# Where the weight sums of the seven-product projections are made: in advance in DRAM, or on POOL as they are used

## The chip, the cores and the metric

The kernel runs on one core of one Trainium2 chip. The metric is the device time of one execution in microseconds (us), the median of three runs. PE is TensorE, DVE is VectorE, ACT is ScalarE, POOL is GpSimd, SP is SyncE, which issues the DMAs here.

## The reference

One inference step of a two-layer trunk, all in float32. The prompt is one sequence of 2048 tokens, the sample is 8 sequences of 8 tokens with stored states; the model width is 1024.

```python
# layer 0: gated DeltaNet (8 heads, 128 x 128 states), chunked
# layer 1: retention
p = rmsnorm(x) @ w_in                       # 1024 -> 1024 q, 1024 k, 2048 v, 2048 gate
q, k = rotary(q), rotary(k) * 256 ** -0.5   # 4 heads, dk 256, dv 512
# per head, chunkwise:  S_t = gamma_h S_{t-1} + k_t^T v_t ;  o_t = q_t S_t
o = rmsnorm(o) * silu(gate)
y = x + o @ w_out
# then a final rmsnorm; outputs: y, and the states of both layers
```

The change touches layer 1 alone, and in it the input projection of q, k, v and gate.

## The kernel before

Layer 0 comes first; it ends near 1500 us. Layer 1 then goes over four blocks of 512 prompt tokens (n = 0 to 3) and, in each, over four heads (h = 0 to 3). Block 0 carries the 64 sample columns as well (width 576). For each head the order of the main line is: gate projection, q, k, then v, then the output projection of the head before (outproj_B), while the retention of the head before (ret_prompt, four chunks of 128 tokens; in block 0 then ret_sample) is interleaved with the gate, q and k projections. The final norm of a block (final) is put after its head 3.

Float32 products are made on PE as three passes of a high and a low part (PASSES). A weight is therefore split before use: ACT copies it to the high part, DVE subtracts to get the low part (split, L209 to L211, or wload for 128x1024 tiles, L195 to L197). Split weights go into a ring of three `w` tiles (wtile), raw ones come through two `wraw` buffers.

Blocks below FIRST7 (0 and 1) project plainly (colproj, pv). From FIRST7 on the projection of two output halves from two input halves, a quad of weight quarters A11, A12, A21, A22, is made with seven products in place of eight. Their right sides are sums of the activations (build_halves: b11, t1, t2, b21, t3, b22, n4; the sums use tags "ta", "tb" and "tc"); their left sides are, in this order, x = 0 (A11), 4 (A21 + A22), 5 (that less A11), 1 (A12), 6 (A11 - A21), 7 (A12 less number 5) and 3 (A22). `seven` puts the products together: two ACT copies, five DVE adds that read PSUM, two POOL adds. A head has four quads of q, k and gate (t = 0 to 3; quad, 12 matmuls of 256 columns for a product) and two of v (t = 4, 5, interleaved; vquad).

The four sums of each quad are made in advance: prep(u), two tasks of low priority (u = 0, 1, half the columns each) that begin after the projections of head 0 in block 0, load each quad, make four sums on POOL, split them (ACT L1055, DVE L1056) and store them to wh_d in DRAM. Each has 24 pieces (4 heads x 6 quads), and before the first build_halves the main line waits for both tasks (pipe.wait(*ptask)). wstream then loads x >= 4 split from wh_d (512 KB each), and x = 0, 1, 3 raw, which it splits.

The order of work has two makers. _Pipe interleaves generator tasks with the main line as the program is written out, by an estimate of PE time and by priority. A planner then orders each engine's instructions by that order of priority and by its own costs, and gives tiles their buffers: tiles of one tag share its buffers, and a buffer passes on when all uses of the former tile are done, those written later included. On the chip each engine, and SP's queue, goes through its list in order.

Tags that matter: in block 0 the pool `pb` holds p0 and p1 (QRs, KRs of the sample), p2 (first vraw, the sample's values, L1548, read by eight small loads at L1257; then K3, written at L1275, read until the last Kts, L1321), raws (raw q and k of the sample). In later blocks p0 to p2 are the second half of the ring of residual tiles (xst, six buffers), taken after pipe.wait(lastret).

Of the kernel before, what the change touches and what calls it, by code (L numbers as in the profile page):

```python
# [10 lines left out]
F32 = mybir.dt.float32  # L11
F32R = mybir.dt.float32r
AF = mybir.ActivationFunctionType
ALU = mybir.AluOpType
# [5 lines left out]
BH = 4  # L20
# [61 lines left out]
class _Layer:  # L82
    pb = None
# [8 lines left out]
def tile_hybrid(ctx: ExitStack, tc: tile.TileContext, a: dict, S: int):  # L92
    nc = tc.nc
    V, ACT, PL = nc.vector, nc.scalar, nc.gpsimd
# [47 lines left out]
    x1_d = dr.tile([D, S + NS], F32, name="x1_d")  # L142
    x2_d = dr.tile([D, S + NS], F32, name="x2_d")
    sr_d = dr.tile([BH, 128, 1024], F32, name="sr_d")
    wh_d = [dr.tile([24, 128, 1024], F32, name=f"wh_d{h}") for h in range(BH)]

    def const(name, shape, src, pool=cst):
        t = pool.tile(list(shape), F32, name=name)
# [26 lines left out]

    def xst(name, wide=True):
        if not wide and xn_[1] == 6:
            k = xn_[2] % 6
            xn_[2] += 1
            if k >= 3:  # L180
                return B.pb.tile([128, TB], F32, tag=f"p{k - 3}", name=name)
        else:
            k = xn_[0] % min(xn_[1], 3 if B.pb else 4)
            xn_[0] += 1
        return (pa if k == 3 else sb).tile([128, XC], F32, tag=f"xst{k}", name=name)
# [829 lines left out]
    def quarters(src, vkind):  # L1015

        if vkind:
            q = [[v3(src[j], 512)[:, :, 256 * i : 256 * i + 256] for i in range(2)] for j in range(2)]
            return q[0][0], q[1][0], q[0][1], q[1][1]
        return [src[j][:, 512 * i : 512 * i + 512] for j in range(2) for i in range(2)]  # L1020
# [16 lines left out]
    def prep(u):  # L1037

        pb = B.pb
        tag = ("ta", "tb")[u]  # L1040
        for h, t in ((h, t) for h in range(BH) for t in range(6)):
            src, vkind = quads(h)[t]
            R = pb.tile([128, 4, 256], F32R, tag=tag, bufs=2, name="Rw")
            Sm = pb.tile([128, 4, 256], F32, tag=tag, bufs=2, name="Sm")
            A11, A12, A21, A22 = (R[:, i, :].bitcast(F32) for i in range(4))
            for x, y in zip((A11, A12, A21, A22), halves_of(src, vkind, u)):
                nc.sync.dma_start(x, y)
            yield 10.0
            PL.tensor_tensor(Sm[:, 0], A21, A22, op=ALU.add)
            PL.tensor_tensor(Sm[:, 1], Sm[:, 0], A11, op=ALU.subtract)  # L1050
            PL.tensor_tensor(Sm[:, 2], A11, A21, op=ALU.subtract)  # L1051
            PL.tensor_tensor(Sm[:, 3], A12, Sm[:, 1], op=ALU.subtract)
            yield 10.0
            with behind():
                ACT.copy(R, Sm)  # L1055
                V.tensor_tensor(Sm.bitcast(F32R), Sm, R.bitcast(F32), op=ALU.subtract)  # L1056
            yield 8.0
            out = wh_d[h][4 * t : 4 * t + 4].rearrange("x p (l v c) -> p x l v c", l=2, v=2)[:, :, :, u, :]
            nc.sync.dma_start(out[:, :, 0], R.bitcast(F32))
            nc.sync.dma_start(out[:, :, 1], Sm)  # L1060
            yield 8.0

    def wstream(h):

        q = quads(h)
        jobs = []
        for ts in ([0], [1], [2], [3], [4, 5]):
            for x in (0, 4, 5, 1, 6, 7, 3):
                jobs += [(t, x) for t in ts]
        for i in range(0, len(jobs), 2):  # L1070
            w, raw = wtile(), None
            for j, (t, x) in enumerate(jobs[i : i + 2]):
                o = w[:, j, :]
                src, vkind = q[t]
                if x < 4:
                    if raw is None:
                        raw = sb.tile([128, 1024], F32, tag="wraw", bufs=2, name="wraw")
                    d = raw[:, 512 * j : 512 * j + 512]
                    nc.sync.dma_start(v3(d, 256) if vkind else d, quarters(src, vkind)[x])
                    split(o[:, :512], o[:, 512:], d)  # L1080
                else:
                    nc.sync.dma_start(o.bitcast(F32), wh_d[h][4 * t + x - 4])
            for j in range(2):
                yield v3(w[:, j, :], 512)

# [97 lines left out]
    def ret_prompt(n, h, QR, KR, Vt, GT, OG, S_):  # L1183
        pb = B.pb
        gC = float(gam[h] ** 128)
        rmask = pb.tile([128, 128], F32, tag="rmk", bufs=2, name="rmk")
        nc.sync.dma_start(rmask, a["rmask"][:, h, :])
        for c in range(4):
            tk = slice(c * 128, (c + 1) * 128)
# [56 lines left out]
    def ret_sample(h, QRs, KRs, vraw, GTs, OG):  # L1246
# [52 lines left out]
        for half in range(2):  # L1299
            o = po("os")  # L1300
            mm(o, Ash[:, half * 128 : (half + 1) * 128], V3[:, half], start=True, stop=False)
            for k in range(2):
                yield LAT_ST
                i0 = 8 * half + 4 * k
                t = pipe.t

                def query(b4):
                    r = slice(32 * b4, 32 * b4 + 32)
                    return mm(o[r], QRs[:, k, half * 128 + 32 * b4 : half * 128 + 32 * b4 + 32], loads[i0 + b4],
                              start=False, stop=(k == 1))  # L1310

                last_in = query(3)
                with tc.issue_after(last_in.ins):
                    for b4 in range(3):
                        query(b4)
                pipe.t = t + 1.0
                for b4 in range(4):
                    i = i0 + b4
                    st = loads[i]
                    Kt = pb.tile([128, 128], F32R, tag=("Kt", "Qc")[b4 % 2], name="Kts")  # L1320
                    ACT.activation(Kt, K3[:, half, k * 128 : (k + 1) * 128].bitcast(F32), AF.Copy,  # L1321
                                   scale=B.kms[:, h, b4 : b4 + 1])
                    yield 0.8
                    p = pc("ps") if b4 % 2 == 0 else pf("ps")
                    mm(p, Kt, V3[:, half])
                    V.scalar_tensor_tensor(st, st, g8, p, op0=ALU.mult, op1=ALU.add)
                    nc.sync.dma_start(a["ret_s"][4 * half + b4, h, k * 128 : (k + 1) * 128, :], st)
                    if i:
                        load(i + ring - 1)
            yield from until(posts[-1])  # L1330
            on = ret_on(o, h, 2)

            def fin(oT, half=half):
                og = pb.tile([128, 4, 32], F32, tag="ogs", name="ogs")
                V.tensor_tensor(og.rearrange("p d (g t) -> p d g t", t=8),
                                oT.rearrange("p d (g s) -> p d g s", s=32)[:, :, :, 0:8],
                                GTs[:, :, 32 * half : 32 * half + 32].rearrange("p d (g t) -> p d g t", t=8),
                                op=ALU.mult)
                cs = slice(TB + 32 * half, TB + 32 * half + 32)
                for d in range(2):  # L1340
                    split(OG[d][:, :, 0, cs], OG[d][:, :, 1, cs], og[:, 2 * d : 2 * d + 2, :])

            post(ret_post(on, fin))
# [225 lines left out]


PIN = False
FIRST7 = 2
LAT_E = 4.0
LAT_SUB = 51.0
LAT_K = 5.5
# [123 lines left out]
```

## Time and profile before

| | us |
|---|---|
| median of 3 runs | 3385.2 (3381.08 to 3391.85) |
| the profiled execution | 3395.24, its span 3393.5 |
| PE busy | 3216.8 (95%) |
| DVE busy | 2357.0 (69%) |
| ACT busy | 1563.8 (46%) |
| POOL busy | 493.7 (15%) |
| PE's share of the chain that ended last | 66% |

Busy times are summed over the span and overlap each other. The mean granted TensorE clock is 0.983 of full speed. V products of block 0 and 1 are called pv in the trace, those of block 2 and 3 sv; the quads' products are sq; plain projections and output projections are pp (from xn or from OG).

### The profile page before, as it was taken

To read this page: it belongs to the slowest core of one execution; us is meant where nothing else is said; L and a number is where in the kernel's file an instruction comes from. 1 tells how busy PE (TensorE), PEld (TensorE's weight loads), DVE (VectorE), ACT (ScalarE), POOL (GpSimd) and SP (SyncE) were. 2 spreads that over 40 slices of the span, in tenths; PEclk is the share of its full clock that TensorE was granted. 3 is DMA by queue.
4 is the path that set the end of the run, shared out by engine and by line. 5 is a ranking of instruction groups with operands and counts; after the bars stand their busy time and mean duration, and the time that the engine had idled before them with its cause. 6 is when DMAs were issued, how large, how long until landed. Compare 5 with 4: busy or idle time off the path is not lost.

```text
span 3393.5 us, 57080 instructions
## 1 busy us (share of the span) xinstructions
PE 3216.8 (95%) x20572; PEld 2769.3 (82%) x20572; DVE 2357.0 (69%) x5218; ACT 1563.8 (46%) x3527; POOL 493.7 (15%) x770
## 2 busy tenths in 40 slices
PE   7999999999999999999999999999969999999997
PEld 6999887778788788788878778688759899889896
DVE  6876878687868868666475766666667567775666
ACT  7655564465435546335243443344344344443443
POOL 1221010001010000011113121222211111011110
PEclk9999999999999999999999999999979999999999
DMA  4333544335443333446767768766678867688665
GB/s 134 94 98 90 175 139 140 125 97 164 128 133 111 95 117 97 139 131 214 246 212 232 238 217 273 244 208 204 199 247 276 273 226 251 228 269 277 222 238 173
DMA packets 408650, 625.60 MB, mean 184 GB/s; under 512 B 119840, under 2 KB 237360, under 8 KB 408368
## 3 DMA queue, kind: packets, MB, share of 16 engines
q1 hardware_dynamic: 408368, 621.96, 57.3%
q8 instruction: 162, 2.65, 0.3%
q14 instruction: 120, 0.98, 0.1%
HBM read 473.04 MB, written 146.68 MB: 183 GB/s over the span
## 4 chain that ended last, share of the span: by engine, by line
PE 66%; DVE 10%; DMA 10%; ACT 6%; issue 4%; POOL 3%; SPq 1%; DVEq 0%; POOLq 0%; ACTq 0%
PE pp L101 37%; PE sq L101 5%; PE pv L101 5%; PE o L101 4%; PE p L101 4%; PE sv L101 3%; PE kyd L101 2%; DMA w<-wh_d 1%; DMA wraw<-in_w_qkg 1%; PE oT L110 1%; DMA x_d<-xr 1%; DVE w L197 1%; DMA wraw<-in_w_v 1%; POOL so L587 1%; DMA out_ret_s<-st 1%
## 5 line engine op out<-in xcount | busy, mean ns | idle before, releaser
L101 PE MATMUL pp<-xn,w 128*128 128x288 f32 (+1 forms) x6224 | 1285.6, 354 | 12.6 <-ACT xn L210 4.7
L101 PEld LDWEIGHTS pp<-xn,w 128*128 128x128 f32 x6224 | 993.4, 189 | 156.2 <-issue 19.3
L101 PE MATMUL pp<-OG,w 128*128 128x512 f32 (+1 forms) x2880 | 589.8, 363 | 35.4 <-DVE xr L1359 28.0
L101 PEld LDWEIGHTS pp<-OG,w 128*128 128x128 f32 x2880 | 487.9, 192 | 119.6 <-DVE xr L1359 28.0
L196 ACT CAST w<-wraw 128x1024 fp32r<-128x1024 f32 x320 | 336.6, 1052 | 383.6 <-PE pp L101 201.5
L197 DVE TENSOR_TENSOR w<-wraw,w 128x1024 fp32r<-128x1024 f32 x320 | 403.0, 1260 | 149.9 <-ACT w L196 141.0
L101 PE MATMUL sq<-xn,w 128*128 128x256 f32 x1536 | 206.2, 284 | 5.8 <-DVE GT L1126 3.3
L101 PEld LDWEIGHTS sq<-xn,w 128*128 128x128 f32 x1536 | 191.4, 188 | 10.4 <-issue 3.8
L101 PE MATMUL pv<-w,xn 128*128 128x512 f32 x768 | 188.5, 398 | 1.9 <-ACT w L196 1.7
L1359 DVE TENSOR_TENSOR xr<-xr,pp 128x512 f32<-128x512 f32 (+1 forms) x160 | 92.4, 592 | 133.6 <-PE pp L101 114.2
L101 PEld LDWEIGHTS pv<-w,xn 128*128 128x128 f32 x768 | 144.2, 189 | 39.5 <-ACT w L196 1.9
L743 DVE SCALAR_TENSOR_TENSOR acc<-pp,cw,acc 128x511 f32<-128x511 f32 (+2 forms) x216 | 160.3, 742 | 20.8 <-ACT acc L740 20.4
L210 ACT CAST w<-wraw 128x512 fp32r<-128x512 f32 x144 | 86.1, 623 | 151.7 <-PE pp L101 50.2
L211 DVE TENSOR_TENSOR w<-wraw,w 128x512 fp32r<-128x512 f32 x144 | 96.9, 688 | 46.7 <-ACT w L210 46.6
L101 PE MATMUL o<-Sc,Qc 128*128 128x512 f32 x360 | 103.1, 411 | 9.0 <-DVE Sc L211 4.7
L1051 POOL TENSOR_TENSOR Sm<-Rw 128x256 f32<-128x256 f32 x48 | 44.0, 917 | 463.9 <-DMA Rw<-in_w_qkg 302.4
L488 DVE TENSOR_TENSOR VP<-VP,tm 128x66 f32<-128x66 f32 (+26 forms) x510 | 106.6, 209 | 4.4
L486 DVE TENSOR_TENSOR tm<-LP,VP 128x66 f32<-128x66 f32 (+26 forms) x510 | 104.6, 205 | 6.1 <-DMA LP<-sl 2.1
L101 PE MATMUL p<-Vh,Kt 128*128 128x512 f32 x384 | 106.7, 409 | 0.7 <-ACT Vh L210 0.7
L1171 POOL TENSOR_TENSOR so<-oss,rsc 128x1 f32<-128x1 f32 x72 | 19.7, 274 | 562.0 <-ACT on L1169 562.0
L110 PE MATMUL oT<-ident,on 128*128 128x128 f32 x432 | 74.7, 280 | 26.8 <-DVE on L588 11.8
L210 ACT CAST OG<-og 128x256 fp32r<-128x256 f32 x192 | 71.7, 405 | 58.8 <-DVE og L643 27.6
(434 smaller groups left out, 5440.5 us busy)
## 6 DMA issues: line engine op xcount, KB each, us to landing
w<-wh_d SPq DMA_DIRECT2D x192, 512.0 KB, 5.6
wraw<-in_w_in_a SPq DMA_DIRECT2D x128, 512.0 KB, 3.5
x_d<-xr SPq DMA_DIRECT2D x160, 256.0 KB, 3.2
wraw<-in_w_qkg SPq DMA_DIRECT2D x64, 512.0 KB, 4.4
xr<-x_d SPq DMA_DIRECT2D x128, 256.0 KB, 4.4
wraw<-in_w_out_b SPq DMA_DIRECT2D x64, 512.0 KB, 4.1
wh_d<-Rw SPq DMA_DIRECT2D x48, 512.0 KB, 3.2
wh_d<-Sm SPq DMA_DIRECT2D x48, 512.0 KB, 3.5
```

Of the source, the lines that this page charges most:

```text
L101: ins = nc.tensor.matmul(out, lhsT, rhs, start=start, stop=stop)
L110: ins = nc.tensor.transpose(out, x, ident[:p, :p])
L196: ACT.copy(w[:, 0, :], raw)
L197: V.tensor_tensor(w[:, 1, :], raw, w[:, 0, :].bitcast(F32), op=ALU.subtract)
L210: ACT.copy(hi, x)
L211: V.tensor_tensor(lo, x, hi.bitcast(F32), op=ALU.subtract)
L486: V.tensor_tensor(tv, LP[:, m, m + 1 : m + 1 + n].unsqueeze(2).to_broadcast([128, n, ncol]), VP[:, m, 0:ncol].unsqueeze(1).to_broadcast([1 ...
L488: V.tensor_tensor(VP[:, m + 1 : m + 1 + n, 0:ncol], VP[:, m + 1 : m + 1 + n, 0:ncol], tv, op=ALU.subtract)
L587: PL.tensor_tensor(so, so, mhalf[:, :2], op=ALU.pow)
L743: V.scalar_tensor_tensor(acc[:, sh:], ap[:, : TB - sh], cw[:, ct, j : j + 1], acc[:, sh:], op0=ALU.mult, op1=ALU.add)
L1051: PL.tensor_tensor(Sm[:, 2], A11, A21, op=ALU.subtract)
L1359: V.tensor_tensor(xs[:, s:e], xs[:, s:e], p[:, : e - s], op=ALU.add)
```

## The change

FIRST7 goes from 2 to 1, so that blocks 1 to 3 use seven products. Prep makes sums for the two v quads of each head alone (t = 4, 5; 8 pieces for each half in place of 24), and wh_d shrinks to 8 tiles a head. For q, k and gate wstream has a new function ready(t): it loads the whole quad into both wraw buffers (two loads of 512 KB), and POOL makes the sums of 128x512 from it: P[0] = A21 + A22, P[1] = P[0] - A11, A21 = A11 - A21 in place, and, once x = 4 is split, P[0] = A12 - P[1]. All seven left sides are then split by ACT and DVE. ready(0) is called when a head's stream begins, ready(t + 1) after the split of x = 3 of quad t. P[0] takes tag "p2" and P[1] tag "raws"; for that the ring of residual tiles goes from six to five buffers, the mask rmk from two to one, and ogs moves to tag "A".

```diff
-    wh_d = [dr.tile([24, 128, 1024], F32, name=f"wh_d{h}") for h in range(BH)]
+    wh_d = [dr.tile([8, 128, 1024], F32, name=f"wh_d{h}") for h in range(BH)]
...
-            k = xn_[2] % 6
+            k = xn_[2] % 5
...
-        for h, t in ((h, t) for h in range(BH) for t in range(6)):
+        for h, t in ((h, t) for h in range(BH) for t in (4, 5)):
...
+        live = {}
+
+        def ready(t):
+
+            r = [sb.tile([128, 1024], F32, tag="wraw", bufs=2, name="wraw") for _ in range(2)]
+            for x, y in zip(r, q[t][0]):
+                nc.sync.dma_start(x, y)
+            P = [B.pb.tile([128, 512], F32, tag=x, name="P") for x in ("p2", "raws")]
+            A11, A12, A21, A22 = quarters(r, False)
+            PL.tensor_tensor(P[0], A21, A22, op=ALU.add)
+            PL.tensor_tensor(P[1], P[0], A11, op=ALU.subtract)
+            PL.tensor_tensor(A21, A11, A21, op=ALU.subtract)
+            live[t] = {0: A11, 4: P[0], 5: P[1], 1: A12, 6: A21, 7: P[0], 3: A22}
+
+        ready(0)
         for i in range(0, len(jobs), 2):
             w, raw = wtile(), None
             for j, (t, x) in enumerate(jobs[i : i + 2]):
                 o = w[:, j, :]
                 src, vkind = q[t]
-                if x < 4:
+                if not vkind:
+                    split(o[:, :512], o[:, 512:], live[t][x])
+                    if x == 4:
+                        PL.tensor_tensor(live[t][7], live[t][1], live[t][5], op=ALU.subtract)
+                    if x == 3 and t < 3:
+                        ready(t + 1)
+                elif x < 4:
...
-        rmask = pb.tile([128, 128], F32, tag="rmk", bufs=2, name="rmk")
+        rmask = pb.tile([128, 128], F32, tag="rmk", bufs=1, name="rmk")
...
-                og = pb.tile([128, 4, 32], F32, tag="ogs", name="ogs")
+                og = pb.tile([128, 4, 32], F32, tag="A", name="ogs")
...
-FIRST7 = 2
+FIRST7 = 1
```

## Rows read from the trace of the kernel before

**Rows 1.** Busy time by stage, from one head's first V product to the next's.

```profile
core 0: us, PE busy (x) PEld busy (x) DVE busy (x) ACT busy (x) POOL busy (x), PEclk, DMA share, GB/s
...
2054.20:2188.90 134.70, 124.83 (x622) 100.58 (x621) 85.14 (x137) 54.50 (x95) 27.04 (x37) 0.96 0.79 256
2188.90:2296.70 107.80, 107.80 (x485) 87.32 (x484) 66.61 (x93) 43.96 (x73) 26.68 (x32) 1.00 0.64 208
2296.70:2405.10 108.40, 108.40 (x490) 87.67 (x488) 69.29 (x95) 45.04 (x75) 25.69 (x32) 1.00 0.66 214
2405.10:2552.10 147.00, 113.04 (x632) 95.80 (x630) 91.75 (x160) 59.77 (x116) 26.61 (x35) 0.87 0.68 223
2552.10:2657.10 105.00, 103.50 (x715) 94.95 (x714) 75.81 (x134) 47.13 (x93) 15.87 (x21) 1.00 0.83 276
2657.10:2760.80 103.70, 101.57 (x701) 93.44 (x701) 65.73 (x117) 41.31 (x84) 13.66 (x20) 1.00 0.71 242
...
2863.90:2976.10 112.20, 105.30 (x704) 95.11 (x703) 84.08 (x163) 51.65 (x109) 12.15 (x18) 0.97 0.73 245
...
3184.30:3288.50 104.20, 101.79 (x702) 93.45 (x701) 65.17 (x115) 41.22 (x84) 12.93 (x19) 1.00 0.70 236
```

**Rows 2.** Busy time by stage, one stretch of the passage from block 1 to 2.

```profile
2470.00:2485.00 15.00, 1.95 (x3) 0.79 (x3) 8.59 (x17) 5.52 (x12) 2.67 (x4) 0.52 0.64 208
```

**Rows 3.** Waits from 2428 to 2507: us in total, times, longest.

```profile
PE pp L101 <- DVE xr L1359: 22.5, 1, 22.5
```

**Rows 4.** Prep's tiles: ns min/median/max, first and last start in us.

```profile
L1056 DVE TENSOR_TENSOR Sm<-Sm,Rw x48: 1212/1220/1760, 1526.5 to 2473.9; 128x1024 fp32r<-128x1024 f32 x48
...
L1060 SPq DMA_DIRECT2D wh_d<-Sm x48: 359/377/1802, 1527.7 to 2475.2; - x48
```

**Rows 5.** Stages: a quad phase, seven-product V, plain V, a wide and a narrow output projection.

```profile
2701.00:2761.00 60.00, 59.28 (x440) 55.69 (x439) 42.25 (x86) 32.00 (x71) 9.54 (x16) 1.00 0.66 226
2761.00:2782.00 21.00, 20.22 (x170) 20.01 (x170) 12.89 (x17) 5.46 (x8) 3.51 (x3) 1.00 0.79 282
1922.00:1951.00 29.00, 29.00 (x123) 22.19 (x122) 26.22 (x44) 11.94 (x21) 8.81 (x8) 0.96 0.80 249
2083.00:2111.00 28.00, 28.00 (x204) 27.31 (x204) 15.93 (x29) 11.08 (x17) 2.66 (x4) 1.00 0.79 254
2679.00:2701.00 22.00, 22.00 (x96) 17.81 (x95) 9.81 (x13) 3.86 (x5) 0.00 (x0) 1.00 0.73 245
```

**Rows 6.** Tiles vraw and K: ns min/median/max, first and last start; the loads' landing.

```profile
L1257 SPq DMA_DIRECT2D r<-vraw x32: 507/588/854, 1575.6 to 2023.0; - x32
...
DMA to landing us min/median/max: 2.0/2.1/4.0
```

```profile
L1321 ACT ACTIVATE Kts<-K,kms x64: 386/402/424, 1590.0 to 2065.5; 128x128 fp32r<-128x128 f32 x64
```

**Rows 7.** Timeline, retention almost alone on PE: start us, us, engine, line, operation.

```profile
2139.70 1.30 PE L101 MATMUL o<-Sc,Qc 128*128 128x512 f32 x5
...
2147.55 2.48 PE L101 MATMUL o<-Sc,Qc 128*128 128x512 f32 x5 [0.20 <-DVE Sc L211]
```

**Rows 8.** DVE and ACT groups of the quad phase 2701 to 2761: busy us, mean ns.

```profile
L211 DVE TENSOR_TENSOR w<-wraw,w 128x512 fp32r<-128x512 f32 x12 | 8.1, 687 | 4.0 <-ACT w L210 4.0
...
L1001 DVE TENSOR_TENSOR QR<-QR,cs 128x512 f32<-128x512 f32 x1 | 0.7, 683 | 0.0
```

```profile
L210 ACT CAST w<-wraw 128x512 fp32r<-128x512 f32 x12 | 7.2, 626 | 5.0 <-PE sq L101 3.2 <-DMA wraw<-in_w_v 1.3 <-DMA wraw<-in_w_qkg 0.6
```

**Rows 9.** POOL's adds: in Vt (whole layer), and groups of the same quad phase.

```profile
L1126 POOL TENSOR_TENSOR Vt<-Vt x16: 1279/1506/2164, 2567.8 to 3306.5; 128x512 f32<-128x512 f32 x16
```

```profile
L1126 POOL TENSOR_TENSOR GT<-GT 128x256 f32<-128x256 f32 x4 | 3.7, 926 | 9.0 <-DVE GT L1126 8.8
...
L1126 POOL TENSOR_TENSOR QR<-QR 128x256 f32<-128x256 f32 x2 | 1.5, 736 | 8.2 <-DVE QR L1126 8.1
```

**Rows 10.** DMA issues from 2573 to 3310: KB each, median us to landing.

```profile
wraw<-in_w_qkg SPq DMA_DIRECT2D x84, 256.0 KB, 4.7
```

More of the change, by code (lines that the diff above doesn't have):

```diff
@@ L1057, in prep @@
             yield 8.0
-            out = wh_d[h][4 * t : 4 * t + 4].rearrange("x p (l v c) -> p x l v c", l=2, v=2)[:, :, :, u, :]
+            out = wh_d[h][4 * t - 16 : 4 * t - 12].rearrange("x p (l v c) -> p x l v c", l=2, v=2)[:, :, :, u, :]
             nc.sync.dma_start(out[:, :, 0], R.bitcast(F32))
@@ L1078, in wstream @@
                     d = raw[:, 512 * j : 512 * j + 512]
-                    nc.sync.dma_start(v3(d, 256) if vkind else d, quarters(src, vkind)[x])
+                    nc.sync.dma_start(v3(d, 256), quarters(src, True)[x])
                     split(o[:, :512], o[:, 512:], d)
                 else:
-                    nc.sync.dma_start(o.bitcast(F32), wh_d[h][4 * t + x - 4])
+                    nc.sync.dma_start(o.bitcast(F32), wh_d[h][4 * t - 16 + x - 4])
             for j in range(2):
```

## Prediction

> **What bounds the kernel now.** I read the page first: PE is busy for 95% of the span, and the chain that ended last is 66% PE. So the question is where PE waits or works too long in the part that the change touches, the retention layer. The second view cuts that layer at the first V product of each head [rows 1]. Read the first column against the PE busy time: a head of block 1 (eight products) takes 107.8 us and PE never rests; a head of block 2 or 3 (seven products) takes 103.4 us where nothing else lies in it (the mean of four, of which the first and the last are shown, 103.7 and 104.2), with some 2 us of PE idle. Two rows stand out: 2405.1 to 2552.1, the passage from block 1 to block 2, takes 147.0 us, and the same passage from block 2 to 3 takes 112.2 us. The third view looks into the long one [rows 2]: in 15 us PE works under 2 us, at a granted clock of 0.52, near the lower of its two levels (1.2 GHz). It waits for the residual adds of the output projection [rows 3], whose loads stand on SP's queue behind loads and stores of prep(). Prep is the reason: its last store is issued at 2475.2 [rows 4], and build_halves(2) takes its buffers "ta" and "tb" only then.
>
> **The passage, first part.** With FIRST7 = 1 blocks 1 to 3 need build_halves, so that now also runs before block 1. Prep shrinks from 48 pieces to 16 (8 for each half). Their 24 pairs went (2475.2 - 1527.7) / 23 = 41 us apart [rows 4], so the eighth ends near 1527.7 + 7 x 41 = 1816 us; build_halves(1) needs the buffers after V of head 3, at 1951. So the stall at 2428 to 2507 goes, and the passage from 1 to 2 becomes like that from 2 to 3: 147.0 - 112.2 = **-34.8 us** [rows 1]. The removed pieces (32 of 1.2 us on DVE, four POOL sums and six DMA issues each) lay beside a busy PE otherwise and are put at nothing; if that cover were gone, they would give a further gain, not a cost.
>
> **Heads 1 to 3 of block 1.** Two clean heads: 107.8 + 108.4 - 2 x 103.4 = **-9.4 us**. The row from 2054.2 takes 134.7 us with 9.9 us of PE idle (prep's loads and the final norm's stores share SP's queue with the weights). After, it is a clean head, 103.4, plus 6 us for the wider output projection (28 against 22 us [rows 5]), plus 2 us for the final norm (105.0 against 103.4 [rows 1]) and 1.6 us for its sample columns, an estimate: 113, so **-21.7 us**.
>
> **Head 0 of block 1.** Here the change adds a wait. The scratch tile P[0] takes tag "p2", one buffer, which in block 0 holds the sample's values (vraw) and then K3. Until now nothing of block 1 touched it before that sample was done; now ready(0) of block 1 asks for it while vraw is still to be read. Before, vraw was read at 2017.6 to 2023.0 and landed 2.1 us later [rows 6]. After, PE comes to the quads near 1980, runs a product or two of raw quarters (x = 0, 1) and then has only the retention of head 3 until vraw is read. Retention alone goes at about 8 us for a chunk of 128 tokens (2139.7 to 2147.6 [rows 7]); one of its four chunks is done by 1980, three more end at 2004, eight small loads and their landing at 2012, a POOL sum of 1.3 and a split of 1.3 at 2014.5. Then 26 products follow at 12 x 20.22 / 170 = 1.43 us [rows 5], 37 us, and about 10 us of sample work: V starts at 2062 instead of 2054.2, **+8 us**. Behind P[0] on POOL wait the two-row sums of `seven` and the `so` pair of the retention.
>
> These four terms give -34.8 - 9.4 - 21.7 + 8 = -58 us, all on PE's path.
>
> **The sums in the quad phase.** Twelve heads now make them. For each quad POOL does four 128x512 sums; ACT and DVE split seven products instead of three. DVE gets 16 subtractions of 0.687 us more for each head [rows 8]: +11.0 us in a phase of 60 us in which it is busy 42.25 [rows 5], so 53. POOL gets 16 sums; the nearest row is its 128x512 add in Vt, 1.28 us at best and 2.16 at worst [rows 9]: +20.6 to +34.6 beside 9.5. ACT rises from 32 to 42. None is over 60, so the cost lies between nothing and what waiting makes of it. Two things speak for a cost.
>
> First, DVE and POOL hold each other up: POOL's add takes 1.28 or 2.16 us, and DVE's 128x1024 subtraction in prep 1.21 or 1.76 [rows 4, 9], the longer ones where both work. If each added sum holds DVE for 0.4 us (an estimate between 0 and that row's 0.54), DVE comes to 53 + 6 = 59 of 60. The densest stretch in which PE did not rest had DVE at 26.22 of 29 us, 0.90 [rows 5]. At full use the phase stays 60; at 0.90 it takes 65.6. The Trainium skill ("SBUF — State Buffer", Practical consequences) says that a DVE instruction with two SBUF inputs and a GpSimd instruction that reads SBUF exclude each other, the second fully blocked; the rows agree in kind (0.88 us more on POOL's add). Its result stands below as a rival.
>
> Second, the chain from quad to quad. The second raw tile comes free only when the last product's split is done, after ACT's 0.626 and DVE's 0.687 [rows 8], 1.3 us; then the load lands after 4.7 us [rows 10], POOL's first sum 1.3 to 2.2 us, a split 1.3 us: 8.6 to 9.5 us and the hops between queues. Three w tiles let weights run six to seven products ahead: 8.6 to 10 us of quads alone, 14.8 us with the retention chunk that lies in each quad (60 / 4). So with a chunk it fits, without one it does not. SP loses 16 of 24 wh_d loads per head (512 KB each) and some 2 us per head in which PE waited can come back.
>
> I take the middle for DVE, between 60 and 65.6, less a little for the lighter DMA: a phase of 62.5, **+2.5 us for each of 12 heads, +30 us**. Bounds: -1 (-12 us, half of PE's waits come back) to +8 (+96 us: each sum holds DVE for the 0.88 us by which POOL's adds differ, 53 + 14 = 67, and 1 us of the chain uncovered).
>
> Edits at nothing: the ring of residual tiles from 6 to 5 (an output projection of 22 us takes 8, one every 2.8 us, so five cover 14 us; were that short, a head would lose up to one tile's 2.8), one mask buffer, ogs on tag "A": small and ahead of their use, hidden by the projections of the head.
>
> **Sum.** -58 + 30 = -28 us. The profiled execution took 3395.2 us (span 3393.5), 0.3% over the median of the runs; I take the -28 to the median: 3385.2 - 28 = **3357 us**. Measurement tells about 0.3%, 10 us, from no change.
>
> **Rivals.**
> *The sums are free* (11%). DVE has 7 us left in the phase and PE has filled its waits before: -58 and up to -12 more, 3315 to 3339. Against it: POOL, ACT and DVE now stand one behind the other.
> *DVE and POOL become the bound* (32%), the one that ends slower. The place is the quad phase, the price 12 us for each microsecond of phase. From +4.8 us the whole gain of 58 is gone, from +5.7 it is slower by 0.3%. For it: DVE at 59 of 60 leaves nothing for in-order waits, and a split that waits for POOL holds up the PSUM reads behind it. With +8 it is 3385 - 58 + 96 = 3423. As a mechanism of this kernel, full exclusion: DVE's two-input work in the phase is 26.9 us (13 rows of DVE, first and last in [rows 8]), after the change 37.9; POOL's is 6.7 (three groups, the first and the last in [rows 9]) + 20.6 = 27.3; together 65.2 us, +5.2 for each phase, 3389 us. That is the page's rule taken to its end; handovers in the rows overlap, so I hold it for less likely than 62.5. I give 8% to no change and 24% to slower.
> *K3 takes the scratch between two quads* (13%). Then quads 1 to 3 of head 0 wait until the sample's last use of K3. Before, that came 2065.5 - 2023.0 = 42 us after vraw's last read [rows 6]; about 25 of them would have no other PE work: 3382. For it: K3 is ready when quad 0 frees the buffer; against it: the quads come earlier in program order. 9% no change, 4% slower.
> *The passage's stall only moves* (7%): build_halves(1), mostly DVE work, meets the output projection and retention, PE falls to half clock as in [rows 2], and 35 us come back before block 1: 3392. Against it: in the passage from block 2 to 3 the same work cost 112.2 - 103.4 = 9 us. 3% and 4%.
>
> **Numbers.** The forecast has 37%; its own range is +1 to +4 us a phase, 3339 to 3375. Faster: 37 + 11 = 48%. No change: 8 + 9 + 3 = 20%. Slower: 24 + 4 + 4 = 32%. The range leaves out the lowest part of the first rival and the top of the second: 3310 to 3425.
>
> **What would show it.** Right: prep ends near 1816; no stretch of half clock between block 1 and 2, a passage of about 112 us; heads of block 1 as long as those of block 2; quad phases of 61 to 64 us with DVE at 53 or more. P[0]'s first sum in block 1 just after the reads of vraw. Wrong: quad phases of 65 us or more, PE waiting for splits that wait for POOL; or a PE gap of over 30 us in head 0 of block 1.

## The result, and the profile of the changed kernel

The changed kernel takes 3516.4 us (3512.9 to 3524.9, four runs) against 3384.6 us for the kernel before on the same chip: a ratio of 1.039, 95% interval 1.0365 to 1.0416. The forecast was 3357 us.

The first view answers to [rows 1]: busy time from one head's first V product to the next's. The first two rows are heads 0 and 1 of block 1, then heads 2 and 3, the passage to block 2, two heads of block 2, the passage to block 3 and the last full head.

```profile
core 0: us, PE busy (x) PEld busy (x) DVE busy (x) ACT busy (x) POOL busy (x), PEclk, DMA share, GB/s
1915.50:2089.10 173.60, 144.23 (x812) 117.37 (x811) 117.57 (x218) 70.57 (x152) 34.65 (x36) 0.87 0.43 141
2089.10:2214.50 125.40, 112.29 (x817) 105.50 (x816) 99.74 (x168) 58.03 (x115) 41.21 (x38) 0.97 0.58 191
2214.50:2333.30 118.80, 106.22 (x702) 96.37 (x701) 82.50 (x131) 50.40 (x100) 37.39 (x34) 0.96 0.44 146
2333.30:2453.10 119.80, 108.11 (x705) 97.97 (x704) 83.83 (x132) 50.48 (x100) 37.22 (x35) 0.94 0.45 148
2453.10:2579.30 126.20, 108.75 (x703) 98.54 (x702) 103.30 (x180) 59.68 (x125) 36.96 (x34) 0.92 0.48 158
2579.30:2697.10 117.80, 106.45 (x714) 96.17 (x713) 93.26 (x151) 55.58 (x109) 41.16 (x37) 0.99 0.55 184
2697.10:2814.70 117.60, 107.06 (x703) 97.55 (x703) 83.85 (x132) 50.40 (x100) 37.49 (x35) 0.94 0.45 149
...
2930.70:3056.70 126.00, 109.11 (x704) 98.97 (x701) 103.86 (x180) 59.79 (x125) 37.49 (x34) 0.92 0.47 158
...
3289.40:3406.70 117.30, 104.81 (x703) 95.23 (x701) 80.70 (x130) 50.23 (x100) 36.53 (x34) 0.97 0.45 146
```

Read the length of each row against that of before. The passage fell from 147.0 to 126.2, but from head 2 of block 1 on every other head grew by 11 to 14 us: 117.6 where [rows 1] has 103.7. PE rests in every row now, 9 to 13 us in a head without a passage. The difference of the two spans, +117.6 us, is made up of block 0, -6.6; heads 0 and 1 of block 1 together, 299.0 against 266.8, +32.2; heads 2 and 3, +22.4; the passage, -20.8; the seven full heads after it, +91.0; the end, -0.6.

The next three views go into one quad phase, 2739 to 2815, the answer to the 60 us of [rows 5]: its window, its groups on DVE and POOL (busy us, mean ns, idle before), and two of its waits (us in total, times, longest).

```profile
2739.00:2815.00 76.00, 65.46 (x443) 60.22 (x442) 59.47 (x102) 39.63 (x85) 28.73 (x28) 0.91 0.29 93
```

```profile
L211 DVE TENSOR_TENSOR w<-wraw,w 128x512 fp32r<-128x512 f32 x17 | 15.2, 910 | 1.3 <-ACT w L210 1.3
L211 DVE TENSOR_TENSOR w<-P,w 128x512 fp32r<-128x512 f32 x10 | 8.7, 875 | 3.9 <-ACT w L210 3.9
L211 DVE TENSOR_TENSOR Sc<-Sr,Sc 128x512 fp32r<-128x512 f32 x8 | 6.7, 847 | 0.0
...
L211 DVE TENSOR_TENSOR Ah<-A,Ah 128x128 fp32r<-128x128 f32 x4 | 2.2, 557 | 0.5 <-ACT Ah L210 0.5
...
L1081 POOL TENSOR_TENSOR wraw<-wraw 128x512 f32<-128x512 f32 x3 | 5.1, 1715 | 0.0
...
L1079 POOL TENSOR_TENSOR P<-wraw 128x512 f32<-128x512 f32 x3 | 4.0, 1322 | 13.4 <-DMA wraw<-in_w_qkg 13.4
```

```profile
ACT w L210 <- POOL P L1079: 6.1, 2, 3.7
...
PEld sq L101 <- DVE GT L1147: 4.8, 2, 2.6
```

DVE's busy time is 59.47 us, which is what the prediction expected (59). But the phase is 76 us long, not 60 to 62.5: no engine is full, PE included (65.46). DVE's subtraction takes 0.91 us in place of 0.687 [rows 8], and the waits are spread over loads, sums, splits and adds that read PSUM. The granted clock, 0.91 in the mean, fell after PE's rests (PE works 0.79 us of 2755 to 2760, and the clock is 0.54 from 2760 to 2765): over the whole run the same 21436 matmuls keep PE busy for 3239.4 us, against 3186.5 in the kernel without sums (below).

One stretch of the same phase, in the timeline (start us, us, engine, line), shows how the engines hold each other up; lines between are left out.

```profile
2776.82 1.30 POOL L1079 TENSOR_TENSOR P<-wraw 128x512 f32<-128x512 f32 x1 [0.78 <-DMA wraw<-in_w_qkg]
...
2777.17 0.48 DVE L1217 SCALAR_TENSOR_TENSOR Kt<-kT,rsc,Kt 128x256 fp32r<-128x256 f32 x1
2777.57 0.28 DVE L1224 TENSOR_TENSOR A<-ap,rmk 128x128 f32<-128x128 f32 x1
2777.77 2.60 DVE L211 TENSOR_TENSOR Sc<-Sr,Sc 128x512 fp32r<-128x512 f32 x2
...
2778.20 1.62 POOL L1080 TENSOR_TENSOR P<-P,wraw 128x512 f32<-128x512 f32 x1
...
2779.78 1.72 POOL L1081 TENSOR_TENSOR wraw<-wraw 128x512 f32<-128x512 f32 x1
...
2780.29 1.36 DVE L211 TENSOR_TENSOR Ah<-A,Ah 128x128 fp32r<-128x128 f32 x1
...
2782.17 0.74 DVE L1147 TENSOR_TENSOR GT<-sq,GT 128x256 f32<-128x256 f32 x2
2782.64 0.99 PE L101 MATMUL sq<-tc,w 128*128 128x256 f32 x6 [2.19 <-DVE GT L1147]
```

DVE's instructions that read one input from PSUM (Kt from kT, A from ap) take their usual time beside POOL's sum. Those with both inputs in SBUF do not: two splits of Sc take 2.60 us (0.68 each alone), one of Ah takes 1.36 (0.29 alone). The adds of `seven` (GT) stand behind them on DVE, and PE waits 2.19 us for these adds, whose inputs none of POOL's weight sums reads or writes.

Head 0 of block 1 shows the scratch tile's wait (windows, then POOL's timeline).

```profile
1982.00:2011.00 29.00, 21.27 (x96) 14.40 (x94) 22.84 (x45) 17.59 (x42) 5.07 (x10) 0.93 0.32 98
2054.00:2076.00 22.00, 10.80 (x36) 4.33 (x35) 9.79 (x19) 6.74 (x18) 2.94 (x4) 0.59 0.57 204
```

```profile
2008.80 1.27 POOL L1079 TENSOR_TENSOR P<-wraw 128x512 f32<-128x512 f32 x1 [5.23 <-DVE V L1281]
...
2073.71 1.26 POOL L1079 TENSOR_TENSOR P<-wraw 128x512 f32<-128x512 f32 x1 [14.91 <-ACT Kts L1342]
```

The first sum comes at 2008.8, just after the last read of vraw (2006.5 and 2.1 us of landing). Then K3 takes the buffer before quad 3, whose first sum waits for the last Kts at 2073.2; PE works 10.8 of 22 us, at a granted clock of 0.59.

### The profile page after: what moved, and what is told of

Same layout as the page of the kernel before. It is cut to its first block, busy times and chain, and to the rows that moved or that the text cites. A ratio compares the mean times of both kernels' runs of the same rounds, so it can differ in the third digit from the quotient of the medians.

```text
span 3511.1 us, 58977 instructions
## 1 busy us (share of the span) xinstructions
PE 3239.4 (92%) x21436; PEld 2830.0 (81%) x21436; DVE 2556.5 (73%) x5518; ACT 1652.6 (47%) x3767; POOL 707.9 (20%) x874
## 4 chain that ended last, share of the span: by engine, by line
PE 53%; DVE 16%; DMA 10%; issue 7%; ACT 7%; POOL 6%; SPq 1%; DVEq 0%; POOLq 0%; ACTq 0%
PE pp L101 27%; PE sq L101 5%; PE sv L101 4%; PE o L101 4%; PE p L101 3%; PE pv L101 3%; PE kyd L101 2%; DMA wraw<-in_w_qkg 2%; DVE w L211 2%; DMA x_d<-xr 2%; DVE Sc L211 1%; DVE w L197 1%; POOL P L1079 1%; DMA wraw<-in_w_out_b 1%; PE oT L110 1%
## 5 line engine op out<-in xcount | busy, mean ns | idle before, releaser
L101 PE MATMUL pp<-xn,w 128*128 128x288 f32 (+1 forms) x5456 | 1096.1, 348 | 10.9 <-ACT xn L210 4.5
L101 PEld LDWEIGHTS pp<-xn,w 128*128 128x128 f32 x5456 | 849.3, 189 | 119.5 <-issue 17.4
L101 PEld LDWEIGHTS pp<-OG,w 128*128 128x128 f32 x2880 | 486.4, 192 | 109.6 <-DVE xr L1380 20.5
L101 PE MATMUL sq<-xn,w 128*128 128x256 f32 x2304 | 338.3, 297 | 58.0 <-DVE GT L1147 23.9
L101 PEld LDWEIGHTS sq<-xn,w 128*128 128x128 f32 x2304 | 309.2, 200 | 73.2 <-ACT w L210 29.2
L211 DVE TENSOR_TENSOR w<-wraw,w 128x512 fp32r<-128x512 f32 x264 | 214.7, 826 | 58.1 <-ACT w L210 57.4
L211 DVE TENSOR_TENSOR w<-P,w 128x512 fp32r<-128x512 f32 x144 | 135.3, 942 | 66.7 <-ACT w L210 65.8
L210 ACT CAST w<-P 128x512 fp32r<-128x512 f32 x144 | 89.0, 622 | 141.5 <-POOL P L1079 95.0
L101 PE MATMUL sv<-w,xn 128*128 128x256 f32 x1152 | 143.7, 282 | 0.7 <-ACT w L210 0.3
L101 PEld LDWEIGHTS sv<-w,xn 128*128 128x128 f32 x1152 | 139.2, 188 | 1.7 <-ACT w L210 0.5
L488 DVE TENSOR_TENSOR VP<-VP,tm 128x66 f32<-128x66 f32 (+26 forms) x510 | 106.7, 209 | 4.4
L101 PE MATMUL sq<-ta,w 128*128 128x256 f32 x576 | 90.7, 306 | 17.7 <-ACT w L210 12.5
```

Of the source, the lines that this page charges most:

```text
L101: ins = nc.tensor.matmul(out, lhsT, rhs, start=start, stop=stop)
L210: ACT.copy(hi, x)
L211: V.tensor_tensor(lo, x, hi.bitcast(F32), op=ALU.subtract)
L488: V.tensor_tensor(VP[:, m + 1 : m + 1 + n, 0:ncol], VP[:, m + 1 : m + 1 + n, 0:ncol], tv, op=ALU.subtract)
```

## The experiments

Each kernel ran once beside the kernel before, unless an interval is given. The kernel before itself took 3381 to 3402 us beside them, so a difference of less than some 15 us between two kernels here tells little. "A clean head" is the mean of the eight periods in which no passage lies (heads 2 and 3 of block 1, three heads each of blocks 2 and 3), from first V product to first V product.

| kernel | time | clean head | DVE busy | POOL busy |
|---|---|---|---|---|
| after | 3516.4 | 117.5 | 2556.5 | 707.9 |
| no sums | 3348.2 | 104.9 | 2438.4 | 419.1 |
| sums on DVE | 3462.5 | 113.8 | 2556.6 | 422.2 |
| raw quads loaded once | 3460.0 | 113.0 | 2562.3 | 702.8 |
| both of these | 3396.3 | 106.7 | 2560.6 | 426.9 |
| sums unread | 3496.8 | 118.6 | 2564.0 | 713.3 |
| fills in place of sums | 3394.5 | 108.7 | 2446.8 | 727.7 |
| 16-column sums | 3411.8 | 110.5 | 2443.5 | 485.5 |
| sums unread, POOL's other work on DVE | 3456.7 | 114.2 | 2604.9 | 529.0 |
| no sums, POOL's other work on DVE | 3339.4 | 103.1 | 2474.9 | 234.3 |
| after, POOL's other work on DVE | 3501.0 | 116.1 | 2596.2 | 521.4 |

**No sums.** What is the change worth without them?

```diff
-            P = [B.pb.tile([128, 512], F32, tag=x, name="P") for x in ("p2", "raws")]
...
-            PL.tensor_tensor(P[0], A21, A22, op=ALU.add)
-            PL.tensor_tensor(P[1], P[0], A11, op=ALU.subtract)
-            PL.tensor_tensor(A21, A11, A21, op=ALU.subtract)
-            live[t] = {0: A11, 4: P[0], 5: P[1], 1: A12, 6: A21, 7: P[0], 3: A22}
+            live[t] = {0: A11, 4: A21, 5: A12, 1: A12, 6: A21, 7: A22, 3: A22}
...
-                    if x == 4:
-                        PL.tensor_tensor(live[t][7], live[t][1], live[t][5], op=ALU.subtract)
```

> The changed kernel with POOL's weight sums left out: products x = 4, 5, 6, 7 take raw quarters, still split by ACT and DVE, so the part left out is the sums themselves, and no scratch tile exists. Measured before: a quad phase of 72 to 76 us against 60. Theory port (DVE and POOL hold each other up and are the bound): the phase falls back to 60 to 63 us, the kernel to about 3516 - 12 x 12 - 28 = 3345 us. Theory chain (the next quad's load waits for the last split of the quad before, then load and split follow in series): only the sum of 1.4 to 1.7 us leaves the chain, the phase stays at 68 to 72 us, the kernel near 3440 us. In either theory the 28 us that head 0 of block 1 costs beyond its phases go, as the scratch tile is gone.

Measured 3348.2 us, 43 less than the 3391.6 of the kernel before beside it and close to the 3345 of the first theory. So the sums and their scratch tile cost 168 us of 3516.4, more than the whole loss (175, if each is taken against the kernel before beside it): 12 heads x 12.6 us make 151, and the scratch tile, which this kernel doesn't use, most of the rest (heads 0 and 1 of block 1: 254.9 us here, 299.0 after; less 2 x 12.6 that is 19 us).

**Which resource: loads, or POOL.** Two kernels change one of them each, a third both: the raw loads are made once for a head, and all four sums go to DVE.

```diff
-            r = [sb.tile([128, 1024], F32, tag="wraw", bufs=2, name="wraw") for _ in range(2)]
-            for x, y in zip(r, q[t][0]):
-                nc.sync.dma_start(x, y)
+            r = live.get("r")
+            if r is None:
+                r = live["r"] = [sb.tile([128, 1024], F32, tag="wraw", bufs=2, name="wraw") for _ in range(2)]
+                for x, y in zip(r, q[t][0]):
+                    nc.sync.dma_start(x, y)
```

> The changed kernel, but a head loads only its first quad of query, key and gate weights; the sums and splits of the three others are made from the same raw tiles, so the part left out is 6 of 8 raw loads of a head. POOL, ACT and DVE do all the work that they do in the changed kernel. Theory port: the phase stays at 70 us or more, the kernel at 3490 or more. Theory chain: without the wait for a free raw tile and the load of 4 to 5 us the phase falls to 61 to 65 us, the kernel to about 3516 - 12 x 10 = 3395 us.

```diff
-            PL.tensor_tensor(P[0], A21, A22, op=ALU.add)
+            V.tensor_tensor(P[0], A21, A22, op=ALU.add)
...
```

> The changed kernel with the four sums of a quad on DVE in place of POOL. DVE gets 16 x 0.69 = 11 us more for each phase. Theory port: no POOL sum shares the port, DVE has 53 + 11 = 64 us without waits, the phase comes to 65 to 68 us, the kernel to about 3430 us. Theory chain: the first sum in the chain takes 0.7 in place of 1.4 to 1.7 us, the phase falls by 3 to 4 us to about 71 us, the kernel to about 3475 us. A third theory, that ACT and DVE stand in order behind POOL's sums: as port, but with no wait of ACT for a sum in the profile.

> Two parts taken together: the sums on DVE, and one raw load for the four quads of query, key and gate (6 of 8 raw loads of a head left out). Alone they gave 3462 and 3460 against 3516. If what they remove adds up, as in a chain in series (load 4 to 5 us, sums 1.4 against 0.7 us each), the phase comes to 62 us and the kernel to about 3405 us. If DVE is the bound (53 + 11 = 64 us of work in the phase), the phase stays at 66 us and the kernel at 3445 us or more.

Measured 3460.0, 3462.5 and, with both, 3396.3 us. Each is worth some 55 us alone, between what the two theories gave; the two together are worth 120, about what a chain in series would have (3405). The table has the point of it: DVE is busy for 2556.5 us when POOL makes the sums and for 2556.6 when DVE makes them all itself. Moving them to POOL takes nothing off DVE. And with DVE equally busy (2562.3 and 2560.6) the kernel that loads once is 64 us slower with POOL's sums: so DVE's busy time alone does not set the time. What does, this pair can't tell, since it changes POOL's reads, its queue and the length of each sum at once.

**Does anyone have to wait for the sums?** My theory was the chain from load to sum to split. Here POOL makes the same four sums into a tile that nobody reads, and the products take raw quarters.

```diff
...
-            live[t] = {0: A11, 4: P[0], 5: P[1], 1: A12, 6: A21, 7: P[0], 3: A22}
+            live[t] = {0: A11, 4: A21, 5: A12, 1: A12, 6: A21, 7: A22, 3: A22, "P": P}
...
```

> The changed kernel in which POOL makes four 128x512 operations on each quad as before, but into a tile that no product reads; products x = 4 to 7 take raw quarters, so the use of the sums is left out. ACT and DVE never wait for a sum, and a load waits for POOL only where POOL still reads the raw tile. Without any sums the kernel took 3348 us, with them 3516. Theory port: DVE is held up by POOL all the same, its busy time in a phase rises by 5 us or more, the phase comes to 66 us or more and the kernel to 3410 or more. Theory waiting (ACT and DVE stand in order behind sums, and the sums lie in series with the load): phases of 60 to 63 us, 3350 to 3370 us.

Measured 3496.8 us: 149 of the 168 remain with nobody waiting for a sum. The 20 us that went lie in heads 0 and 1 of block 1 (278.2 us in place of 299.0), where this kernel has no scratch tile to wait for; a clean head is no shorter (118.6 against 117.5). So in the clean heads the wait for the sums costs nothing that shows beside what else they do, and as the cause my chain falls. Two others were left: POOL's reads beside DVE's, and POOL's queue (the retention's row factor `so` and two adds of `seven` stand behind up to 6 us of sums). Of the waits of its phase 2719 to 2794 the first speaks for the reads, the second for the queue.

```profile
PE sq L101 <- DVE GT L1147: 8.9, 2, 6.7
...
ACT on L1194 <- POOL so L1193: 5.4, 3, 4.9
```

**Queue, reads and chain, each alone.** Fills keep POOL as busy with hardly a read (three more stand after x = 4, in a part that is left out here):

```diff
-            PL.tensor_tensor(P, A21, A22, op=ALU.add)
-            PL.tensor_tensor(P, P, A11, op=ALU.subtract)
-            PL.tensor_tensor(P, A11, A21, op=ALU.subtract)
+            PL.tensor_tensor(P[:, :16], A21[:, :16], A22[:, :16], op=ALU.add)
+            for _ in range(9):
+                PL.memset(P, 0.0)
```

> The kernel with sums that nobody reads (3497 us), with the four sums of each quad replaced by one 16-column sum and twelve fills of a 128x512 tile with zero, which read nothing and keep POOL busy for about as long (12 x 0.53 = 6.4 us a quad, nine ahead and three after x = 4). The products take raw weights. If the cost is POOL's queue (the retention's row factors and the adds of the seven products stand behind 5 us of other work): 3470 to 3500, phases of 72 to 75 us. If the cost is that POOL's reads and DVE's two-input instructions hold each other up: 3350 to 3380, phases of 61 to 63 us, DVE's subtraction at some 0.70 us.

The next keeps the reads and takes everything away that could wait behind them; and its control does so without sums (both with the other edits of their base kernels, left out here):

```diff
-        add(PL, c[0][1], c[0][1], c[1][1])
-        add(PL, c[1][1], c[1][0], c[1][1])
+        add(V, c[0][1], c[0][1], c[1][1])
+        add(V, c[1][1], c[1][0], c[1][1])
...
-        PL.tensor_tensor(so, ss, B.rsc[:, h, col : col + 1], op=ALU.add)
-        PL.tensor_tensor(so, so, mhalf[:, :1], op=ALU.pow)
+        V.tensor_tensor(so, ss, B.rsc[:, h, col : col + 1], op=ALU.add)
+        V.reciprocal(so, so)
```

> The kernel with sums that nobody reads (3497 us), with the work that stood behind them on POOL moved to DVE: the add for the retention's row factor (its root is left out, a reciprocal stands in its place) and the two adds of the seven products that POOL made. Now nobody waits for POOL in a quad phase, but POOL reads as much as before. If the cost is POOL's queue: 3360 to 3400, phases of 62 to 64 us. If it is the two engines holding each other up: 3470 or more, phases of 70 us or more, with DVE's busy time at 60 or more of them, since DVE has the moved work too (some 5 us a phase).

> The kernel without POOL's sums (3348 us), with the work moved from POOL to DVE as in the run with unread sums (the add for the retention's row factor, its root left out, and the two adds of the seven products). It is the control of that run, which took 3457 us: the difference between the two is what POOL's reads alone cost, since nobody waits for POOL in either. If POOL's reads beside DVE's are the cost: 3340 to 3365 us, heads of 105 to 106 us. If it was DVE's 5 us of added work in each phase: 3420 or more, heads of 111 us or more.

And sums of 16 columns (the other three in the same way, left out here) keep a chain and little else. It is not quite the chain of the changed kernel: as the sums are made in place, three of them also wait for the split of x = 0 or x = 1.

```diff
+            c = slice(0, 16)
+            PL.tensor_tensor(A21[:, c], A21[:, c], A22[:, c], op=ALU.add)
+            live[t] = {0: A11, 4: A21, 5: A11, 1: A12, 6: A22, 7: A12, 3: A22}
```

> The kernel after, with POOL's four sums of each quad cut to 16 of 512 columns, made in place on the raw quarters, in the same order and behind the same loads; the other columns of the left sides are raw weights. So the chain load, POOL, split stays, with its hops between queues, and POOL's time on it is nearly gone. Left: 3348 us is the kernel without sums, 3516 the kernel after. If it is POOL's occupancy (its reads beside DVE's, or its queue) that costs 13 us a phase: 3350 to 3375, quad phases of 61 to 63 us. If it is the chain of hops from quad to quad: 3440 or more, phases of 68 us or more, with waits of splits for POOL's sums.

Fills: 3394.5 us, +46 over no sums (3.8 a clean head), between the two theories: alone, the queue costs something, not most. Reads: 3456.7, a little under the 3470 expected of them, against a control of 3339.4, which fits its first expectation: **+117 us** (114 if each is taken against the kernel before beside it), or 11.1 of the 12.6 us of a clean head, the largest part; DVE's busy time grows by 130.0 us for the same 5782 instructions, 0.68 us for each of 192 sums. 16-column sums: 3411.8, +64 (5.6 a clean head), also between. The first line of the four pages (busy time, share, instructions: control, reads, no sums, fills) shows what reads do and writes don't do to DVE:

```profile
PE 3185.7 (95%) x21436; PEld 2797.9 (84%) x21436; DVE 2474.9 (74%) x5782; ACT 1645.7 (49%) x3767; POOL 234.3 (7%) x418
```

```profile
PE 3213.9 (93%) x21436; PEld 2813.1 (81%) x21436; DVE 2604.9 (75%) x5782; ACT 1642.8 (48%) x3767; POOL 529.0 (15%) x610
```

```profile
PE 3186.5 (95%) x21436; PEld 2793.5 (83%) x21436; DVE 2438.4 (73%) x5518; ACT 1643.4 (49%) x3767; POOL 419.1 (13%) x682
```

```profile
PE 3200.4 (94%) x21436; PEld 2805.8 (83%) x21436; DVE 2446.8 (72%) x5518; ACT 1646.8 (49%) x3767; POOL 727.7 (21%) x1306
```

The same quad phase (block 2, head 2) in the control and with the reads:

```profile
2649.00:2708.00 59.00, 58.90 (x436) 55.23 (x436) 52.24 (x114) 39.08 (x85) 0.00 (x0) 1.00 0.34 110
```

```profile
2703.00:2774.00 71.00, 62.22 (x447) 57.66 (x446) 60.86 (x116) 38.83 (x85) 18.48 (x12) 0.98 0.30 98
```

In the control DVE is busy for 0.89 of the phase and PE never rests. So a DVE that is busy for so much of the time is not by itself the trouble. With the reads the same work takes it 8.6 us longer and the phase 12 us longer: what stands behind a stopped instruction waits too.

**After, with the queue cleared.** The same move of POOL's other work, with the sums in use:

> The kernel after (sums used) with the same work moved from POOL to DVE: the add for the retention's row factor (root left out, a reciprocal in its place) and the two adds of the seven products. Its splits still wait for the sums. If POOL's queue is the cost: 3380 to 3430, of which the rest is the chain from load to sum to split; phases of 62 to 66 us. If the engines hold each other up: 3500 or more, phases as long as after (72 to 76 us).

Measured 3501.0: only 15 of 3516.4 saved, and the control gained 9 by the same move. This fits the second expectation. Against the control a clean head takes 13.0 us more (116.1 against 103.1), as much as the sums cost with the queue (12.6). So beside the reads the queue adds nothing that shows.

**The scratch tile.** P[0] of head 0 in block 1 gets another buffer:

```diff
...
+            if own:
+                P = [sb.tile([128, XC], F32, tag="xst2", name="P")[:, :512]] + P
```

> The changed kernel, but in head 0 of block 1 the scratch tile P[0] takes a residual buffer (xst2) in place of the one that vraw and K3 hold. Theory scratch: the two holes of PE in that head (1982 to 2011, before vraw is read, and 2054 to 2076, until the last use of K3) go; from its first V product the head comes from 173.6 us to about 131 + 13 = 144 us, the kernel to about 3516 - 29 = 3487 us. Rival: the holes belong to the retention and the sample and would be there anyway: 3510 us or more.

Measured 3511.8, a total that fits the rival. Head 0 takes 144.0 us as the theory had it, but head 1 takes 139.5 (125.4 after), since part of the sample's work now falls there: 283.5 for the two against 299.0. In this run the part ahead of the retention layer's first V product took 8.0 us longer and head 1 of block 2 took 6.1 longer, so of the 15.5 us hardly any is left in the total. Why those two were longer is not known.

**The kernel before with earlier sums.** If prep is what made the passage long, it need not go; it need only be done in time. First all of it at a pace meant to end before block 1, with seven products from block 1 on; then only the pace changed a little. Each yield stands in two places, and the lag between the two tasks goes from 18 to 8 and to 15.5.

```diff
-            yield 10.0
+            yield 5.0
...
-            yield 8.0
+            yield 3.0
...
-FIRST7 = 2
+FIRST7 = 1
```

> The kernel before with FIRST7 = 1 alone and all 24 pieces of prep for each half kept, at a pace of 16 us in place of 36, so that they end before block 1. No sum is made in the quad phase and no scratch tile is used. The three terms of the prediction that did not depend on the sums (-34.8, -9.4, -21.7 us) should show alone: about 3385 - 66 = 3319 us if the faster prep hides in block 0; 3340 to 3360 us if prep's 32 further pieces there (1.2 us of DVE and 3 to 4 us of POOL each) cost PE 1 us each. A rival, that the stall moves to the passage into block 1: about 3385 us.

```diff
-            yield 10.0
+            yield 9.0
...
-            yield 8.0
+            yield 6.5
```

> The kernel before with nothing but prep's pace changed: 31 us of the pipe's time for a piece in place of 36. Its 24 pieces for each half then end near 1528 + 23 x 36 = 2360 us in place of 2475, ahead of the passage from block 1 to 2. If the stall of that passage was prep's, it falls from 147.0 to about 112 us: 3385 - 35 = 3350 us, with eight products in block 1 and no sum made in place. If the passage is long for another reason (the first build_halves, the weights' first loads), it stays: 3380 to 3390 us.

The first takes 3468.7 us, a ratio of 1.0233 (1.0216 to 1.025). Prep did not end in time there: its last store is issued at 2072.8, and the same stall stands in the passage into block 1, which grows from 132.1 to 204.5 us. One wait makes most of it (waits from 1976 to 2181: us in total, times, longest).

```profile
PE pp L101 <- DVE xr L1359: 49.3, 1, 49.3
```

The three heads ahead of it are 55 us longer too, and the later heads give back less (from V of head 1 of block 1 to V of head 0 of block 2: 316.1 against 363.2 us). So the rival that the stall moves is right here, and what seven products from block 1 on would gain with prep in time stays untested. The second takes 3359.0 us against 3392.5, **0.9911 (0.989 to 0.9931)**, and beats both kernels. Its passage to block 2, which was 147.0 us, in the profiled execution (the fastest of five, 3342.1 us; the others took 3357.5 to 3364.7):

```profile
2402.00:2507.60 105.60, 103.88 (x631) 91.40 (x630) 79.73 (x155) 51.98 (x110) 9.05 (x16) 1.00 0.70 226
```

PE hardly rests and the clock stays full. Its last store of sums is issued at 2411.7 in place of 2475.2 [rows 4]; 2360 was expected.

## Why the prediction was wrong

**The passage, -34.8.** Right. The kernel without sums has 114.7 us there, -32.3; after has 126.2, 11.5 more, about what the sums add to every head. Prep's last split is at 1853 (1816 forecast), well ahead of its use, and the faster pace of prep alone brought 105.6.

**Heads 2 and 3 of block 1, -9.4.** Right: 103.8 + 105.1 against 216.2 us, -7.3 without sums.

**Heads 0 and 1 of block 1, -21.7 and +8.** Half right. Without sums and scratch the two give -11.9, not -21.7. The missing 10 us are in head 1: the forecast made it a clean head and let its 9.9 us of PE idle go with prep's loads, but they stay. The row without sums, to be read against that from 2054.2 in [rows 1], has 124.0 us in place of 113, with 9.7 us of PE idle.

```profile
2049.00:2173.00 124.00, 114.35 (x839) 104.83 (x838) 95.05 (x176) 60.61 (x121) 18.66 (x24) 1.00 0.68 223
```

The scratch tile's wait came where and in the order that was forecast, but costs 16 to 21 us, not 8 (299.0 against 283.5 with a buffer of its own, and against 278.2 with the sums unread, which use no p2): K3 took the buffer before quad 3, the third rival, held at 13%.

**The quad phase, +2.5 us a head.** This is the step that failed: "I take the middle for DVE, between 60 and 65.6 ... a phase of 62.5". The term is 12.6 us a head, 151 in all, where +30 was taken and +96 was the upper bound. Even without the sums a head takes 104.9 us in place of the forecast's 103.4. Both mechanisms, DVE and POOL holding each other up and the chain, were named; their sizes and the way to a time were wrong, in three places.

- Each sum lengthens DVE's work by 0.62 us (118.1 / 192, after less no sums), where 0.4 was estimated. That alone would have been 3.4 us a phase. The trace of before had the sign of it: beside prep's smaller sums (128x256, 0.74 to 0.80 us in the median), a split of 0.29 us already took up to 0.84.

```profile
L211 DVE TENSOR_TENSOR Ah<-A,Ah x64: 278/292/835, 1531.2 to 3341.0; 128x128 fp32r<-128x128 f32 x64
```

- The rule that DVE costs nothing at 0.90 of a phase took a stopped instruction for a busy one. DVE runs at 0.89 in the control and PE never rests; in the changed kernel DVE is at 0.78 (59.47 of 76) and PE rests for 10.5 us. The same holds of the rival with full exclusion, 65.2 us a phase (65.1, as 16 x 1.28 is 20.5): it added up two engines' busy times and left out the instructions behind the stopped one. So the bound of +8 us a phase was too low, and with it the range's upper end. (The range, 3310 to 3425, leaves out no part of the rivals as they were priced, 3315 to 3423, though the prediction says that it does.) The tiles' durations after (ns min/median/max) show how hard the exclusion is: a split with two inputs in SBUF (Ah, Sc) grows by up to 1.1 us, most of a sum, whatever its own size; an instruction with one input in PSUM (Sr) does not grow.

```profile
L211 DVE TENSOR_TENSOR Ah<-A,Ah x64: 277/291/1357, 1530.8 to 3458.0; 128x128 fp32r<-128x128 f32 x64
...
L211 DVE TENSOR_TENSOR Sc<-Sr,Sc x120: 674/684/1787, 1555.8 to 3457.4; 128x512 fp32r<-128x512 f32 x120
L1251 DVE SCALAR_TENSOR_TENSOR Sr<-Sr,p x120: 669/680/689, 1559.8 to 3464.2; 128x512 f32<-128x512 f32 x120
```

The Trainium skill ("SBUF — State Buffer", Who interferes with whom) states just this: two SBUF inputs on DVE contend with a GpSimd instruction that reads SBUF, not with one that only writes it, and one with at most one SBUF input does not contend outside the 2-port modes. The trace agrees (Sc up to 1.79 us, Sr at most 0.69), and the fills (DVE 2446.8 us against 2438.4) agree on the writes.

- The chain from quad to quad was put at 1 us at most. With 16-column sums it costs 64 us, 5.6 a clean head (POOL is still 66 us busier there, and some sums wait for splits that the changed kernel's don't wait for), and taking six of eight raw loads away from the changed kernel saves 56. Queue (46), chain (64) and reads (117) add up to 227, more than the 168 that they cost together, so they cover each other in part. In a clean head the reads alone make 11.1 of the 12.6 us, and taking away the wait for the sums (118.6 against 117.5) or the queue (13.0 against 12.6) gives nothing back. What queue and chain would cost together without the reads, no run shows.

A third of the sums' cost comes through PE's clock: against the kernel without sums PE's busy time grows by 52.9 us for the same matmuls, as the mean granted clock falls from 0.986 to 0.968, and its rest by 112.

Not settled: what keeps PE idle for those 9.7 us in head 1 of block 1 once prep is out of the way.

## What to carry to other kernels

Before work is moved to an engine that "has time", look at what it reads and where: here POOL's sums, which read SBUF, held up DVE's instructions with both inputs in SBUF (0.29 us became up to 1.36), and what waits is DVE's whole list behind them. Here the move freed no DVE time at all (2556.5 us with the sums on POOL, 2556.6 on DVE). Price such a move by the instructions queued behind the stopped one, not by busy shares; and where prepared work only comes too late, try its pace first: a change of pace alone gave 0.9% here, while a faster pace together with seven products one block earlier, where the sums again came too late, cost 2.3%.

## What the runs showed of the hardware that was not expected

- A DVE split of 0.29 us with both inputs in SBUF (Ah) takes up to 1.36 us beside a POOL sum of 128x512, and one of 0.68 (Sc) up to 1.79; POOL's own sum varies from 1.26 to 1.84 us.
- POOL's fills of 128x512 (some 0.53 us each, 12 for each quad) hardly lengthen DVE's work: 2446.8 us against 2438.4, with POOL busy for 727.7 us.
- In the control DVE is busy for 0.89 of a quad phase in which POOL does nothing, and PE works for 58.90 of its 59 us.
